# A third load buffer, chained key products and transposes, and a second bank for a gate, in a four-layer float32 kernel

## The chip, the cores and the metric

The kernel runs on one core of a Trainium2 chip. Its time is the device time of one execution in microseconds (us). The time before is the median of three runs, and one further execution was recorded by the hardware profiler; the rows below come from that one.

## The reference

Two blocks of two layers each are computed in float32 for 512 tokens of width 1024. The change touches mostly the first layer. It normalises the input, multiplies it with one wide matrix, and feeds the columns to a windowed attention and to a state space mixer; the outputs are gated, joined and projected.

```
def even_layer(hn, ...):
    q, k, v, gate_a, u, gate_b = split_cols(hn @ w_in, EVEN_SPLITS)   # 512,128,128,512,512,512
    q = rms_norm(q.reshape(bsz, L, 8, 64), q_g); k = rms_norm(k.reshape(bsz, L, 2, 64), k_g)
    att = swa_sink_attention(q, k, v, sinks, rel_bias) * silu(gate_a)
    ssm = s5_mixer(u, log_dt, a_re, ..., d_skip, glu_w, glu_b) * silu(gate_b)
    return concatenate([att, ssm], -1) @ w_out

def s5_mixer(u, ...):
    ab, f from exp(log_dt), a_re, a_im;  bb = f * b               # small complex tables
    x = associative_scan of x[l] = ab * x[l-1] + bb u[l]          # 32 groups, 64 states
    y = gelu(re(c x) + d_skip * u)
    h = y @ glu_w + glu_b
    return h[..., :512] * sigmoid(h[..., 512:])
```

The later layers are a top-k attention (layer 2), an attention with forget gates and one with dilated windows (layers 3 and 4, function `attn34`), the last two each followed by a convolutional feed-forward block. Between every two of these stands `h = h + out` and a root mean square norm.

## The kernel before

Each float32 product is made of three products of rounded parts (`mm3`, lines 227 to 229 and, through a `Chain`, line 361): a weight is loaded to a tile `raw` (line 211), ScalarE writes the rounded part `wh` (line 216), VectorE or GpSimd the remainder `wl` (line 217). `slab` does this for 8 x 128 rows by 256 columns in two parts. Tiles of one tag share a fixed number of buffers: two of `raw`, two pairs of `wh` and `wl`, two PSUM banks `acc`. `ring["lo"] = G` gives the remainder of a slab's second part to GpSimd in the state space stage.

The program is written in order, but a planner fixes the order of instructions on each engine from its own model of their lengths, by priority in the order of the text; `urgent` raises the priority. The engines then run their lists in order and wait on semaphores. `tc.issue_after(ins)` fixes that the instructions in its block stand behind `ins` on that engine; `Chain` does so for each TensorE instruction that passes through it, and so writes out an order by hand.

The first stage runs so: `norm_half(0)` normalises token blocks 0 and 1 (VectorE line 266 in two halves, then eight transposes on TensorE, line 288, and the split of the result, lines 291 and 292), with a few products on zeros that keep TensorE busy (`keep_warm`). `kv_half(0)` makes keys and values of these 256 tokens, turns them (line 505), normalises the keys (`head_norm`, lines 440 to 445, with a power on GpSimd, line 251), and turns them again (line 511). `norm_half(1)` and `kv_half(1)` follow for blocks 2 and 3, with the small tables of the state space model on VectorE between them. Then the products for `u2` (line 647), and the state space mixer in four quarters: `core_a(qu)` (lines 659 to 742; VectorE makes `zb`, lines 675 to 677, TensorE turns and multiplies it, VectorE makes `c7`, line 715, TensorE uses that at line 722) and `core_b(qu)` (lines 744 to 805; a scan on VectorE with the table `et`, TensorE's `yp`, line 780, then a gelu). The table `et` is built by doubling in `cmul_pow` (lines 571 to 574). The query products and the gates' products (`silu2`) stand behind in the text and fill TensorE in between as far as the planner puts them there.

The attention of layer 1 (lines 1050 to 1075) goes through units of a token block and a key head: `l1_scores`, one or two `glu_piece`s, `l1_values`, `l1_turn`. All its TensorE work but the norms' transposes goes through one `Chain`. `glu_piece(n)` makes half a gated unit in the PSUM bank `misc`, of which there is one: the even `n` end in a tanh on ScalarE (line 920), the odd ones in line 926 on VectorE. `finish` writes the output projection in quarters to `misc` (the last block's first half to `o`), then `norm_block` normalises the block, and four steps later its eight transposes are written, to the banks `misc` and `tps`, the last block's later still. `attn34` uses the same `finish` and chain; layer 2 uses `finish` without a chain.

Of the kernel before, what the change touches and what calls it, by code (L numbers as in the profile page):

```python
# [8 lines left out]
F32 = mybir.dt.float32  # L9
# [88 lines left out]
def _build(tc, nc, ctx, t, out, dbg, upto):  # L98
# [90 lines left out]

    ring = {"n": 0, "extra": None, "lo": V}  # L190

# [3 lines left out]

    def slab(src, r0, kc, pieces, wpool=None, parts=None):

        n = sum(p[1] for p in pieces)
        per = max(1, 1024 // n)
        pl = wpool  # L200
        if pl is None:
            ring["n"] += 1
            pl = ring["extra"] if ring["extra"] and ring["n"] % 3 == 0 else wp
        hi = pl.tile([128, WSZ], F32R, tag="wh", name="wh")[:, :kc * n].rearrange("p (k n) -> p k n", n=n)
        lo = pl.tile([128, WSZ], F32R, tag="wl", name="wl")[:, :kc * n].rearrange("p (k n) -> p k n", n=n)
        def part(k0, k1):
            raw = rawp.tile([128, 1024], F32, tag="raw", name="raw")[:, :(k1 - k0) * n].rearrange(
                "p (k n) -> p k n", n=n)
            o = 0
            for c0, w in pieces:  # L210
                nc.sync.dma_start(raw[:, :, o:o + w],
                                  src[r0 + k0 * 128:r0 + k1 * 128, c0:c0 + w].rearrange("(k p) n -> p k n", p=128))
                o += w
            eng = G if ring["lo"] is G and k0 > 0 else V
            with urgent() if evq[1] else nullcontext():
                A.activation(hi[:, k0:k1], raw, AF.Copy)  # L216
                eng.tensor_tensor(lo[:, k0:k1], raw, hi[:, k0:k1].bitcast(F32), op=OP.subtract)  # L217
        for k0 in range(0, kc, per):
            f = lambda k0=k0: part(k0, min(kc, k0 + per))
            if parts is None:  # L220
                f()
            else:
                parts.append(f)
        return hi, lo
# [56 lines left out]

    def to_x(xn, hdst, ldst, nk=8, tags=("tps", "tps"), view=lambda a: a):

        for half in range(nk // 4):
            ps = pst(tags[half])
            pv = ps.rearrange("p (k t) -> p k t", k=4)
            for k in range(4):
                turned[0] = PE.transpose(pv[:, k], xn[:, (half * 4 + k) * 128:(half * 4 + k + 1) * 128], ident).ins
# [5 lines left out]
    def norm_block(hb, gb, x, tb, tags=("tps", "tps"), pl=None, put_off=None):  # L294
        xn = (pl or nrm).tile([128, 1024], F32, tag="xn", name="xn")
        norm_scale(hb, gb, xn)
        sl = slice(tb * 128, (tb + 1) * 128)

        def rest():
            to_x(xn, lambda hf: x.h[hf][:, :, sl], lambda hf: x.l[hf][:, :, sl], tags=tags)  # L300
        if put_off:
            put_off(rest)
        else:
            rest()
# [142 lines left out]

    w = slab(w_in1, 0, 8, [(512, 256)])
    tmp = nrm.tile([128, 1024], F32, tag="xn", name="tmp")
    br = tmp[:, :512].rearrange("p (r g i) -> p r g i", r=2, g=16)  # L450
    for i, nm in enumerate(("ev_ssm_b_re", "ev_ssm_b_im")):
        for q in range(2):
            nc.sync.dma_start(br[q * 64:(q + 1) * 64, i],
                        t[nm][0].rearrange("(q g) p i -> q p g i", q=2)[q])
    crow = tmp[:, 512:].rearrange("p (r f x) -> p r f x", r=2, f=2)
    for i, nm in enumerate(("ev_ssm_c_re", "ev_ssm_c_im")):
        for hf in range(2):
            nc.sync.dma_start(crow[:, i, hf].rearrange("r (q p) -> r q p", q=2),
                              t[nm][0].rearrange("(q f g) o p -> f (g o) q p", q=2, f=2)[hf])
    mkd = pp.tile([128, 16], F32, name="mkd")  # L460
    nc.sync.dma_start(mkd, t["maskd"])
    qg = cst.tile([128, 4], F32, name="qg")
    for i, nm in enumerate(("ev_q_norm_g", "ev_k_norm_g")):
        for q in range(2):
            nc.sync.dma_start(qg[q * 64:(q + 1) * 64, i:i + 1], t[nm].rearrange("o d -> d o"))
    for i, nm in enumerate(("od_q_norm_g", "od_k_norm_g")):
        nc.sync.dma_start(qg[:, 2 + i:3 + i], t[nm].rearrange("o d -> d o"))
    qgs = cst.tile([128, 4], F32, name="qgs")
    V.tensor_copy(qgs, qg)
    V.tensor_scalar(qgs[:, 0:1], qg[:, 0:1], -0.125, None, op0=OP.mult)  # L470
    V.tensor_scalar(qgs[:, 2:3], qg[:, 2:3], -float(np.float32(128 ** -0.5)), None, op0=OP.mult)
    normed = []
# [12 lines left out]
    def norm_half(half):  # L485
        for tb in (2 * half, 2 * half + 1):
            normed.append(norm_block1(xin[tb], gb, x1, tb, n0, normed[-1] if normed else None))
            if half == 0:
                with tc.issue_after(turned[0]):
                    keep_warm(4)  # L490

    def kv_half(half):
        kvf = []
        for part in range(2):
            ps = acc()
            fm(ps[:, :256].rearrange("p (i j) -> p i j", i=4), w, part * 128, 128, xhalf(x1, half))
            f_ = n0.tile([128, 256], F32, tag=f"kvf{part}", name="kvf", bufs=1)
            evac(by_i(f_), ps[:, :256].rearrange("p (i j) -> p i j", i=4))
            kvf.append(f_)
        for q in range(2):  # L500
            tb = 2 * half + q
            sl = slice(tb * 128, (tb + 1) * 128)
            ps = sps()
            for part in range(2):
                PE.transpose(ps[:, part * 128:(part + 1) * 128], kvf[part][:, q * 128:(q + 1) * 128], ident)
            kn2 = pj.tile([128, 2, 2, 64], F32, tag="kn2", name="kn2", bufs=2)
            head_norm(ps[:, :128], 2, 64, [kn2[:, :, r] for r in range(2)])
            evac(vt[:, tb], ps[:, 128:256])
            tp = pst("ft")
            for i in range(2):  # L510
                PE.transpose(tp[:, i * 128:(i + 1) * 128], kn2[:, i].rearrange("p a d -> p (a d)"), ident)
            A.activation(kT[:, :, sl], tp[:, :256].rearrange("p (a t) -> p a t", a=2), AF.Copy, scale=qgs[:, 1:2])

    norm_half(0)

    def ctile():
# [7 lines left out]
    prmps = sps()  # L524
    with tc.issue_after(turned[0]):
# [103 lines left out]

    def bias_read(dst, h0, nh, m0, n):  # L630
# [6 lines left out]

    pst_.close()

# [243 lines left out]
    evq[1], ring["lo"] = False, V  # L883
    ssx.close()
# [25 lines left out]
    def glu_piece(n):  # L910
# [844 lines left out]
```

## Time and profile before

| | us |
|---|---|
| median of three runs | 1863.38 (1863.2 to 1865.21) |
| the profiled execution | 1865.96 |
| its span, first to last instruction | 1864.2 |
| TensorE busy in it | 1782.7 |
| mean granted clock of TensorE in it, 1 being full | 0.983 |

The span is what the views below divide; 1.8 us lie around it. Busy times of the engines overlap, so they do not add up to the span. The clock is granted at one of two levels, 1.0 or 0.5 of full speed, and a window's value is a mean of both.

### The profile page before, as it was taken

The page shows a single profiled execution, that of the slowest core. Times are in us where ns is not written, and L with a number is a line of the kernel's source. Part 1 is how long each engine was busy: PE and PEld are TensorE (multiplying, and loading weights), DVE is VectorE, ACT ScalarE, POOL GpSimd, SP SyncE. Part 2 cuts the span into 40 slices and gives each one's busy share as a digit, 9 for nine tenths or more (in the row PEclk, how much of TensorE's full clock was granted, in tenths as well). Part 3 has the DMA queues.
Part 4 walks back from the last instruction along what each step waited for, and adds up shares of the span by engine and source line. Part 5 has one row for each costly group of instructions (what it writes and reads, how often), then busy time and mean ns, then how long its engine had stood idle before and what let it go on. Part 6 is the DMA issues. An engine that isn't in the chain of part 4 may idle for free.

```text
span 1864.2 us, 27803 instructions
## 1 busy us (share of the span) xinstructions
PE 1782.7 (96%) x11134; PEld 1507.9 (81%) x11136; DVE 1036.1 (56%) x2110; ACT 735.8 (39%) x1460; POOL 152.5 (8%) x160
## 2 busy tenths in 40 slices
PE   7899899999999999899999999999999899999998
PEld 5777689878689886788888888889967888888886
DVE  6865475279855525655655562266466455555522
ACT  5333353353444335544433342233355344333421
POOL 3432101222120000000000000000000000000000
PEclk8889999999999999999999999999999999999999
DMA  5303222312513233003333323333410133332221
GB/s 166 117 12 109 96 91 64 91 58 68 163 46 120 84 116 97 1 2 104 112 92 91 91 74 118 103 125 96 132 46 1 37 113 99 103 93 80 101 91 68
DMA packets 187897, 161.73 MB, mean 87 GB/s; under 512 B 14568, under 2 KB 170320, under 8 KB 187768
## 3 DMA queue, kind: packets, MB, share of 16 engines
q1 hardware_dynamic: 181168, 144.30, 24.9%
q0 software_dynamic: 2784, 9.00, 1.6%
q10 hardware_dynamic: 3816, 6.66, 1.0%
q8 instruction: 88, 1.44, 0.3%
q14 instruction: 41, 0.34, 0.1%
HBM read 157.88 MB, written 4.74 MB: 87 GB/s over the span
## 4 chain that ended last, share of the span: by engine, by line
PE 74%; DVE 12%; ACT 4%; issue 4%; DMA 3%; POOL 2%; POOLq 0%; DVEq 0%; SPq 0%; ACTq 0%
PE acc L227 19%; PE acc L229 19%; PE acc L228 18%; PE misc L361 6%; PE o L361 3%; DVE wl L217 2%; PE tps L361 1%; PE spp L361 1%; ACT wh L216 1%; DVE isc L1198 1%; ACT p L1517 1%; PE misc L227 1%; DVE xn L266 1%; POOL rstd L251 1%; PE misc L228 1%
## 5 line engine op out<-in xcount | busy, mean ns | idle before, releaser
L217 DVE TENSOR_TENSOR wl<-raw,wh 128x1024 fp32r<-128x1024 f32 (+3 forms) x242 | 294.2, 1225 | 375.1 <-ACT wh L216 374.6
L216 ACT ACTIVATE wh<-raw 128x1024 fp32r<-128x1024 f32 (+2 forms) x262 | 270.2, 1044 | 490.4 <-PE acc L228 200.5
L227 PE MATMUL acc<-xh,wh 128*128 128x512 f32 (+2 forms) x1064 | 401.2, 379 | 3.9 <-ACT xh L291 3.9
L228 PE MATMUL acc<-xl,wh 128*128 128x512 f32 (+2 forms) x1064 | 401.0, 377 | 0.0
L229 PE MATMUL acc<-xh,wl 128*128 128x512 f32 (+2 forms) x1064 | 400.0, 376 | 0.0
L227 PEld LDWEIGHTS acc<-xh,wh 128*128 128x128 f32 (+1 forms) x1064 | 199.8, 189 | 43.7 <-ACT xh L291 4.6
L229 PEld LDWEIGHTS acc<-xh,wl 128*128 128x128 f32 (+1 forms) x1064 | 200.4, 188 | 39.2
L228 PEld LDWEIGHTS acc<-xl,wh 128*128 128x128 f32 (+1 forms) x1064 | 200.4, 188 | 38.4 <-DVE xl L292 0.2
L227 PE MATMUL acc<-wh,xh 128*128 128x256 f32 (+1 forms) x704 | 204.7, 291 | 1.6 <-ACT xh L291 1.4
L229 PE MATMUL acc<-wh,xl 128*128 128x256 f32 (+1 forms) x704 | 201.2, 286 | 0.8 <-DVE xl L292 0.8
L228 PE MATMUL acc<-wl,xh 128*128 128x256 f32 (+1 forms) x704 | 200.1, 285 | 0.0
L227 PEld LDWEIGHTS acc<-wh,xh 128*128 128x128 f32 x704 | 134.9, 192 | 9.8 <-issue 6.2
L229 PE MATMUL acc<-wh,gl 128*128 128x512 f32 x352 | 139.2, 395 | 0.0
L227 PE MATMUL acc<-wh,gh 128*128 128x512 f32 x352 | 138.5, 394 | 0.0
L228 PE MATMUL acc<-wl,gh 128*128 128x512 f32 x352 | 138.5, 393 | 0.0
L229 PEld LDWEIGHTS acc<-wh,xl 128*128 128x128 f32 x704 | 135.1, 192 | 1.4 <-DVE xl L292 1.2
L228 PEld LDWEIGHTS acc<-wl,xh 128*128 128x128 f32 x704 | 135.0, 192 | 0.2 <-issue 0.2
L264 POOL TENSOR_TENSOR rs<-ss,mhalf 128x1 f32<-128x1 f32 x32 | 17.7, 553 | 1398.8 <-DVE ss L262 1323.4
L361 PE MATMUL misc<-wh,ah 128*128 128x256 f32 x280 | 81.9, 293 | 3.6 <-DVE xl L292 2.2
L361 PE MATMUL misc<-wh,al 128*128 128x256 f32 x280 | 79.6, 284 | 2.0 <-DVE al L1556 2.0
L361 PE MATMUL misc<-wl,ah 128*128 128x256 f32 x280 | 79.0, 282 | 0.0
L228 PEld LDWEIGHTS acc<-wl,gh 128*128 128x128 f32 x352 | 66.1, 188 | 15.6
(1383 smaller groups left out, 3064.9 us busy)
## 6 DMA issues: line engine op xcount, KB each, us to landing
raw<-in_w_up_dram SPq DMA_DIRECT2D x176, 256.0 KB, 3.2
raw<-in_w_down_dram SPq DMA_DIRECT2D x44, 512.0 KB, 3.5
raw<-in_od_w_in_dram SPq DMA_DIRECT2D x24, 512.0 KB, 3.4
raw<-in_w_in_dil_dram SPq DMA_DIRECT2D x20, 512.0 KB, 3.6
raw<-in_ev_w_in_dram SPq DMA_DIRECT2D x18, 512.0 KB, 3.6
raw<-in_w_out_dram SPq DMA_DIRECT2D x16, 512.0 KB, 3.3
raw<-in_w_in_fox_dram SPq DMA_DIRECT2D x14, 512.0 KB, 4.1
raw<-in_ev_w_out_dram SPq DMA_DIRECT2D x8, 512.0 KB, 3.6
```

The lines of the kernel that those rows point to most:

```text
L216: A.activation(hi[:, k0:k1], raw, AF.Copy)
L217: eng.tensor_tensor(lo[:, k0:k1], raw, hi[:, k0:k1].bitcast(F32), op=OP.subtract)
L227: pe.matmul(ps, lh, rh, start=first, stop=False)
L228: pe.matmul(ps, lh, rl, start=False, stop=False)
L229: pe.matmul(ps, ll, rh, start=False, stop=last)
L251: G.tensor_tensor(r2[:, :n], r[:, :n], mhalf[:, :n], op=OP.pow)
L264: G.tensor_tensor(r, ss[:, 3:4], mhalf[:, :1], op=OP.pow)
L266: last = V.scalar_tensor_tensor(xn[:, hv[i]], hb[:, hv[i]], r, gb[:, hv[i]], op0=OP.mult, op1=OP.mult)
L361: self.last = op(*a, **k).ins
L1198: V.match_replace(out=s_, in_to_replace=m8_, in_values=s_, imm_value=-3e38)
L1517: A.activation(p2, src, AF.Exp, bias=nm[:, hd:hd + 1], scale=-1.0, accum_out=sm[:, hd:hd + 1])
```

## The change

Four things are done. In the state space stage each third part of a weight slab is loaded to a `raw` tile of a pool of its own (`rawx`); to make room, the pool `prep` is closed earlier, `mkd` and the key halves move to the pool `pj`, and the tanh of `silu2` shares the buffer `s_` of the gelu. The key slab's two splits are written behind `norm_half(0)`, and its remainders on VectorE stand behind the norm of block 1; `kv_half(1)`'s products, the first four `u2` products, and between those the turns and norms of `kv_half(1)` go through a chain `c1`. `glu_piece` 1 and 3 use the bank `o`. Where `finish` has a chain, the norms' transposes go through it and use two `tps` banks.

```
+    ring = {"n": 0, "extra": None, "lo": V, "raw": None, "rn": 0}
 ...
         def part(k0, k1):
-            raw = rawp.tile([128, 1024], F32, tag="raw", name="raw")[...]
+            ring["rn"] += 1
+            raw = (ring["raw"] if ring["raw"] and ring["rn"] % 3 == 0 else rawp).tile([128, 1024], ...)[...]
 ...
                 A.activation(hi[:, k0:k1], raw, AF.Copy)
-                eng.tensor_tensor(lo[:, k0:k1], raw, hi[:, k0:k1].bitcast(F32), op=OP.subtract)
+                with tc.issue_after(lo_after()) if lo_after else nullcontext():
+                    eng.tensor_tensor(lo[:, k0:k1], raw, hi[:, k0:k1].bitcast(F32), op=OP.subtract)
 ...
-    w = slab(w_in1, 0, 8, [(512, 256)])
+    kvparts = []
+    w = slab(w_in1, 0, 8, [(512, 256)], parts=kvparts, lo_after=lambda: normed[1])
+    ...
+    c1 = Chain()
+    def kv_half(half):
+        kvf, kn = [], {}
+        for part in range(2):
+            ps = acc()
+            fm(..., w, part * 128, 128, xhalf(x1, half), pe=c1 if half else PE)
+            f_ = pj.tile([128, 256], F32, tag="qn", name="kvf", bufs=2)
+            evac(by_i(f_), ...)
+            kvf.append(f_)
+        pe = c1 if half else PE
+        def norm(q):    # two transposes through pe, head_norm, evac of the values
+        def turn(q):    # two transposes through pe, ScalarE to kT
+        return [lambda: norm(0), lambda: norm(1), lambda: turn(0), lambda: turn(1)]
+    norm_half(0)
+    for f in kvparts:
+        f()
 ...
-    kv_half(0)
+    for f in kv_half(0):
+        f()
     norm_half(1)
 ...
-    kv_half(1)
+    kv_rest = kv_half(1)
 ...
+    pst_.close()
     ysx = ExitStack()
 ...
+    ring["raw"] = phase(ssx, "rawx")
 ...
-            tm(ps[:, :256], w, xk(x1, i * 128, i * 128 + 128))
+            tm(ps[:, :256], w, xk(x1, i * 128, i * 128 + 128), pe=c1)
+            if kv_rest:
+                kv_rest.pop(0)()
             evac(u2[:, cs_ * 16:(cs_ + 1) * 16, i, :], ...)
 ...
-        th_ = pl.tile([128, 512], F32, tag="th", name="th_", bufs=1)
+        th_ = pl.tile([128, 512], F32, tag="s_", name="s_")
 ...
-        w, ps = glu_w[cs_], pst("misc")
+        w, ps = glu_w[cs_], pst("o" if n in (1, 3) else "misc")
 ...
-                norm_block(h[:, tb], gb, x, tb, ("misc", "tps"), pl, lambda f: steps.later(4, f))
+                norm_block(h[:, tb], gb, x, tb, ("tps", "tps") if chain else ("misc", "tps"), pl,
+                           lambda f: steps.later(4, f), chain or PE)
```

## Rows read from the trace of the kernel before

**Rows 1.** The page's part 1: engine, busy us, share of the span, instructions.
```profile
PE 1782.7 (96%) x11134; PEld 1507.9 (81%) x11136; DVE 1036.1 (56%) x2110; ACT 735.8 (39%) x1460; POOL 152.5 (8%) x160
```

**Rows 2.** Windows: stretch, its length, busy us of PE, PEld, DVE, ACT, POOL, PEclk, DMA, GB/s.
```profile
45.00:52.00 7.00, 3.97 (x10) 1.20 (x11) 5.84 (x20) 2.28 (x6) 1.73 (x2) 0.71 0.43 143
52.00:76.00 24.00, 23.77 (x191) 23.48 (x191) 23.69 (x25) 4.47 (x9) 17.86 (x17) 0.94 0.37 112
76.00:82.00 6.00, 0.54 (x4) 0.35 (x3) 5.86 (x12) 3.18 (x5) 0.98 (x1) 0.72 0.51 170
...
113.00:130.00 17.00, 17.00 (x95) 14.36 (x94) 7.77 (x16) 3.48 (x6) 5.81 (x5) 0.50 0.00 1
...
222.00:226.00 4.00, 4.00 (x13) 2.88 (x11) 0.98 (x3) 0.00 (x0) 0.00 (x0) 0.57 0.00 0
```

**Rows 3.** Waits of PE from 0 to 232 us: us in total, times, longest.
```profile
PE tps L722 <- ACT bt L707: 5.5, 1, 5.5
PE ft L511 <- DVE kn L445: 3.6, 1, 3.6
```

**Rows 4.** Timeline of DVE: start, us, engine, line, operation, tiles, [idle before, releaser].
```profile
13.28 1.22 DVE L217 TENSOR_TENSOR wl<-raw,wh 128x1024 fp32r<-128x1024 f32 x1 [1.20 <-ACT wh L216]
...
15.67 1.23 DVE L217 TENSOR_TENSOR wl<-raw,wh 128x1024 fp32r<-128x1024 f32 x1 [0.56 <-ACT wh L216]
16.81 0.75 DVE L266 SCALAR_TENSOR_TENSOR xn<-xin,rs,gb 128x512 f32<-128x512 f32 x1
```

**Rows 5.** Timeline of PE, the first half's key products, first after the restart and last.
```profile
20.80 0.39 PE L228 MATMUL acc<-xl,wh 128*128 128x256 f32 x1
...
26.30 0.28 PE L229 MATMUL acc<-xh,wl 128*128 128x256 f32 x1
```

**Rows 6.** Timeline of DVE from 33 to 82 us: table doubling, two splits, the tile c7.
```profile
33.98 0.21 DVE L571 TENSOR_TENSOR ctmp<-pw 128x32 f32<-128x32 f32 x1
...
52.71 3.94 DVE L571 TENSOR_TENSOR ctmp<-et 128x32 f32<-128x32 f32 x1
...
65.39 5.41 DVE L571 TENSOR_TENSOR ctmp<-et 128x256 f32<-128x256 f32 x1
...
72.90 1.22 DVE L217 TENSOR_TENSOR wl<-raw,wh 128x1024 fp32r<-128x1024 f32 x1
...
81.41 0.28 DVE L715 TENSOR_TENSOR c<-sps,dm 128x128 f32<-128x128 f32 x1
```

**Rows 7.** Timeline of ACT from 78 to 82 us.
```profile
78.56 1.06 ACT L216 ACTIVATE wh<-raw 128x1024 fp32r<-128x1024 f32 x1 [8.80 <-DMA raw<-in_ev_w_in_dram]
...
81.11 1.08 ACT L707 ACTIVATE bt<-tps 128x512 f32<-128x512 f32 x2
```

**Rows 8.** Timeline of PE, the starts of gated-unit pieces 1 and 3.
```profile
221.42 0.51 PE L361 MATMUL misc<-yh,wh 128*128 128x512 f32 x1 [2.56 <-ACT th__2201 L920]
...
232.66 0.50 PE L361 MATMUL misc<-yh,wh 128*128 128x512 f32 x1 [1.73 <-ACT th__2259 L920]
```

**Rows 9.** Timeline of PE, two quarters of layer 1's output projection behind transposes.
```profile
299.90 0.38 PE L361 MATMUL misc<-wh,ah 128*128 128x256 f32 x1 [1.32 <-DVE ss L261]
...
313.39 0.39 PE L361 MATMUL misc<-wh,ah 128*128 128x256 f32 x1 [0.97 <-DVE xl L292]
```

**Rows 10.** Timeline of PE in layers 3 and 4, transposes of the norm and what follows.
```profile
790.10 0.66 PE L288 MATMUL tps<-ident,xn 128*128 128x128 f32 x4 [1.50 <-ACT pt__7978 L381]
792.00 0.55 PE L361 MATMUL misc<-wh,ah 128*128 128x256 f32 x1 [1.24 <-DVE xl L292]
...
842.13 0.55 PE L288 MATMUL tps<-ident,xn 128*128 128x128 f32 x3 [3.88 <-DVE xn L266]
...
1475.17 0.90 PE L288 MATMUL tps<-ident,xn 128*128 128x128 f32 x3 [3.88 <-DVE xn L266]
```

**Rows 11.** Timeline of DVE at 790 and 842 us.
```profile
790.94 0.41 DVE L379 COPY pt__7983<-tps 128x256 f32<-128x256 f32 x1
...
841.99 0.68 DVE L1556 TENSOR_TENSOR al<-o,ah 128x512 fp32r<-128x512 f32 x1
```

More of the change, by code (lines that the diff above doesn't have):

```diff
@@ L187, in urgent, with slab @@
         return tc.high_priority()
-    ring = {"n": 0, "extra": None, "lo": V}
+    ring = {"n": 0, "extra": None, "lo": V, "raw": None, "rn": 0}
     def ring_start(extra):
         ring["n"], ring["extra"] = 2, extra
-    def slab(src, r0, kc, pieces, wpool=None, parts=None):
+    def slab(src, r0, kc, pieces, wpool=None, parts=None, lo_after=None):
         n = sum(p[1] for p in pieces)
@@ L206, in part @@
         def part(k0, k1):
-            raw = rawp.tile([128, 1024], F32, tag="raw", name="raw")[:, :(k1 - k0) * n].rearrange(
+            ring["rn"] += 1
+            raw = (ring["raw"] if ring["raw"] and ring["rn"] % 3 == 0 else rawp).tile([128, 1024], F32, tag="raw", name="raw")[:, :(k1 - k0) * n].rearrange(
                 "p (k n) -> p k n", n=n)
@@ L280, in _build, with to_x @@
     turned = [None]
-    def to_x(xn, hdst, ldst, nk=8, tags=("tps", "tps"), view=lambda a: a):
+    def to_x(xn, hdst, ldst, nk=8, tags=("tps", "tps"), view=lambda a: a, pe=PE):
         for half in range(nk // 4):
@@ L287, in to_x @@
             for k in range(4):
-                turned[0] = PE.transpose(pv[:, k], xn[:, (half * 4 + k) * 128:(half * 4 + k + 1) * 128], ident).ins
+                turned[0] = pe.transpose(pv[:, k], xn[:, (half * 4 + k) * 128:(half * 4 + k + 1) * 128], ident)
             pv = view(pv)
@@ L292, in to_x, with norm_block @@
             V.tensor_tensor(ldst(half), pv, h_.bitcast(F32), op=OP.subtract)
-    def norm_block(hb, gb, x, tb, tags=("tps", "tps"), pl=None, put_off=None):
+    def norm_block(hb, gb, x, tb, tags=("tps", "tps"), pl=None, put_off=None, pe=PE):
         xn = (pl or nrm).tile([128, 1024], F32, tag="xn", name="xn")
@@ L446, in head_norm @@
                                 r.rearrange("p (h o) -> p h o", o=1).to_broadcast([128, nh, dh]), op=OP.mult)
-    w = slab(w_in1, 0, 8, [(512, 256)])
[L449 to L471, printed above, removed]
+    kvparts = []
+    w = slab(w_in1, 0, 8, [(512, 256)], parts=kvparts, lo_after=lambda: normed[1])
     normed = []
@@ L488, in norm_half @@
             if half == 0:
-                with tc.issue_after(turned[0]):
+                with tc.issue_after(turned[0].ins):
                     keep_warm(4)
+    c1 = Chain()
     def kv_half(half):
-        kvf = []
+        kvf, kn = [], {}
         for part in range(2):
             ps = acc()
-            fm(ps[:, :256].rearrange("p (i j) -> p i j", i=4), w, part * 128, 128, xhalf(x1, half))
-            f_ = n0.tile([128, 256], F32, tag=f"kvf{part}", name="kvf", bufs=1)
+            fm(ps[:, :256].rearrange("p (i j) -> p i j", i=4), w, part * 128, 128, xhalf(x1, half), pe=c1 if half else PE)
+            f_ = pj.tile([128, 256], F32, tag="qn", name="kvf", bufs=2)
@@ L498, in kv_half @@
             evac(by_i(f_), ps[:, :256].rearrange("p (i j) -> p i j", i=4))
             kvf.append(f_)
-        for q in range(2):
-            tb = 2 * half + q
-            sl = slice(tb * 128, (tb + 1) * 128)
+        pe = c1 if half else PE
+        def norm(q):
             ps = sps()
             for part in range(2):
-                PE.transpose(ps[:, part * 128:(part + 1) * 128], kvf[part][:, q * 128:(q + 1) * 128], ident)
+                pe.transpose(ps[:, part * 128:(part + 1) * 128], kvf[part][:, q * 128:(q + 1) * 128], ident)
@@ L506, in kv_half @@
             kn2 = pj.tile([128, 2, 2, 64], F32, tag="kn2", name="kn2", bufs=2)
             head_norm(ps[:, :128], 2, 64, [kn2[:, :, r] for r in range(2)])
-            evac(vt[:, tb], ps[:, 128:256])
+            evac(vt[:, 2 * half + q], ps[:, 128:256])
+            kn[q] = kn2
+        def turn(q):
+            sl = slice((2 * half + q) * 128, (2 * half + q + 1) * 128)
             tp = pst("ft")
             for i in range(2):
-                PE.transpose(tp[:, i * 128:(i + 1) * 128], kn2[:, i].rearrange("p a d -> p (a d)"), ident)
+                pe.transpose(tp[:, i * 128:(i + 1) * 128], kn[q][:, i].rearrange("p a d -> p (a d)"), ident)
@@ L512, in kv_half @@
             A.activation(kT[:, :, sl], tp[:, :256].rearrange("p (a t) -> p a t", a=2), AF.Copy, scale=qgs[:, 1:2])
+        return [lambda: norm(0), lambda: norm(1), lambda: turn(0), lambda: turn(1)]
     norm_half(0)
+    for f in kvparts:
+        f()
+    tmp = nrm.tile([128, 1024], F32, tag="xn", name="tmp")
+    br = tmp[:, :512].rearrange("p (r g i) -> p r g i", r=2, g=16)
+    for i, nm in enumerate(("ev_ssm_b_re", "ev_ssm_b_im")):
+        for q in range(2):
+            nc.sync.dma_start(br[q * 64:(q + 1) * 64, i],
+                        t[nm][0].rearrange("(q g) p i -> q p g i", q=2)[q])
@@ new lines, in _build @@
+    crow = tmp[:, 512:].rearrange("p (r f x) -> p r f x", r=2, f=2)
+    for i, nm in enumerate(("ev_ssm_c_re", "ev_ssm_c_im")):
+        for hf in range(2):
+            nc.sync.dma_start(crow[:, i, hf].rearrange("r (q p) -> r q p", q=2),
+                              t[nm][0].rearrange("(q f g) o p -> f (g o) q p", q=2, f=2)[hf])
+    mkd = pj.tile([128, 16], F32, name="mkd")
+    nc.sync.dma_start(mkd, t["maskd"])
+    qg = cst.tile([128, 4], F32, name="qg")
+    for i, nm in enumerate(("ev_q_norm_g", "ev_k_norm_g")):
+        for q in range(2):
+            nc.sync.dma_start(qg[q * 64:(q + 1) * 64, i:i + 1], t[nm].rearrange("o d -> d o"))
@@ L516, in ctile @@
+    for i, nm in enumerate(("od_q_norm_g", "od_k_norm_g")):
+        nc.sync.dma_start(qg[:, 2 + i:3 + i], t[nm].rearrange("o d -> d o"))
+    qgs = cst.tile([128, 4], F32, name="qgs")
+    V.tensor_copy(qgs, qg)
+    V.tensor_scalar(qgs[:, 0:1], qg[:, 0:1], -0.125, None, op0=OP.mult)
+    V.tensor_scalar(qgs[:, 2:3], qg[:, 2:3], -float(np.float32(128 ** -0.5)), None, op0=OP.mult)
     def ctile():
@@ L524, in _build @@
     prmps = sps()
-    with tc.issue_after(turned[0]):
+    with tc.issue_after(turned[0].ins):
         for i in range(3):
@@ L882, in _build @@
             silu2(sp_, gat[:, cs_ * 2 + q], ps)
-    evq[1], ring["lo"] = False, V
+    evq[1], ring["lo"], ring["raw"] = False, V, None
     ssx.close()
```

3 lines of the change are left out of this document (1 added, 2 removed).

## The prediction

> **What bounds the kernel now.** I read the page's busy shares first: TensorE is busy 96% of the span [rows 1], so an edit can only give back its idle time and the stretches at half clock. The windows come second. The reader should see that the idle time lies in few places: in 45 to 52 us TensorE works 3.97 of 7 us, and in 76 to 82 us 0.54 of 6, and that between these two VectorE is busy 23.69 of 24 us, with GpSimd at work in 17.86 of them [rows 2]. From 113 to 130 us TensorE is busy throughout, at a clock of 0.50. Third come the waits of TensorE, which name what ends the gaps: 5.5 us for the tile `bt` at line 722 and 3.6 us for `kn` at line 511 [rows 3]. The timelines of VectorE and ScalarE tell why those were late [rows 4, 6, 7], and TensorE's own timeline shows the gated unit and the transposes [rows 8 to 10]. All times are of the profiled execution, 1865.96 us, of which 1.8 lie around the span; it is 2.6 us above the median of 1863.38. I take the savings from it and subtract the same microseconds from the median.
>
> **The change part by part.**
>
> *The key slab behind the norms.* The norm's second half for block 1 stands at 16.81 us behind two remainders of 1.22 and 1.23 us, which themselves waited 1.20 and 0.56 us for ScalarE [rows 4]: 4.2 us that the order now moves behind it. The second remainder still ends at 15.67 + 1.23 = 16.90, since its data bound it, and the key products resume at 20.80 [rows 5]. With the norm out of the way they can resume near 16.9, up to 3.9 us earlier. Nothing is added; the slab's loads stay next to the inputs' on SP's queue, as no other load is written between. What may take the gain back is ScalarE's list, if a later split stands ahead of the next blocks' transposes there. So 0 to 3.9; I take 3, near the upper end, because the row's waits are plain and the products that follow run without gap from 20.80 to 26.30 [rows 5].
>
> *The second half's keys in a chain with the first `u2` products.* The 3.6 us wait for `kn` at line 511 [rows 3] blocked `u2` products that were ready; now two or three blocks of them stand between a norm and its turn. The clock in that window is 0.71, so of its 3.97 busy us some 3.97 x 0.29 = 1.2 are lost too [rows 2]: 4.8 at most. The new risk is the chain itself: if `kn` is late once more, the products queued behind it wait, at the price of the same row, 3.6. But the products then finish early in front of a VectorE that is full until 82 us [rows 2], and only what TensorE takes from its later work in the time won counts. So from -4.8 to +3.6; I take -2. The closing of `prep`, the new place of `mkd` and of the key halves cost nothing as instructions: the same ones run on the same engines. The shared buffer of `silu2` lets no gate go before the last gelu; the queries, not the gates, fill that time today.
>
> *The third load buffer.* ScalarE waited 8.80 us for a load, until 78.56, and the eviction of `bt` stood behind it at 81.11 [rows 7]. That load waited for a `raw` buffer, freed by the remainder that VectorE reached at 72.90 [rows 6]; with a third buffer the first part of the slab is there long before. The second part takes an old buffer and still waits for that remainder. What is late next is `c7`: it ends at 81.41 + 0.28 = 81.69 us [rows 6], and line 722 reads it also. If VectorE keeps its list, the 5.5 us are worth 0.1. If the planner, which sees the products of `u2` end earlier, moves `c7` ahead of the remainder and of the tables before it, all 5.5 and the half clock in 76 to 82 us [rows 2] may go, some 7. A third buffer adds no instruction, so below nothing there is only contention among loads, and the loads' share is 0.37 and 0.51 there [rows 2]. I take 3, in the middle, as the row does not tell what the planner does.
>
> *The second bank for pieces 1 and 3 of the gated unit.* Both waited for the tanh of the piece before, 2.56 and 1.73 us [rows 8], and behind the first the clock fell: 4.00 us at 0.57, 4.00 x 0.43 = 1.7 lost [rows 2]. Together 6.0. Piece 3 now waits for line 926 of piece 1, a score and a whole piece 2 earlier, and the first values for that of piece 3, a score and a piece earlier; that work covers both. If VectorE is late there, one of the waits stays and the gain is 2.6. I take 5.5.
>
> *The transposes in the chains.* In layer 1 two quarters of the projection waited 1.32 and 0.97 us for transposes to leave `misc` [rows 9]. They now leave `tps`, which no turn needs any more at that point: 2.3 gained. In layers 3 and 4 the largest waits, 3.88 us each [rows 10], are for a norm of the next block; but the product that follows needs `al`, which VectorE makes at 841.99 [rows 11], so it could start 0.1 us earlier at most, at 842.67, and the gap stays. In the other place the transposes waited 1.50 us for one `tps` bank; the second of the two banks is free only at 790.94 + 0.41 = 791.35 [rows 11], 1.25 us later than they started, while the 1.24 us behind them [rows 10] go. These cancel. So for layers 3 and 4 I take 0, between 5 us gained (3.88 once, with a clock that stays up) and 7.5 lost (1.25 for each of the six blocks there that pass the chain).
>
> Sum: 3 + 2 + 3 + 5.5 + 2.3 = 15.8, say 16 us: 1865.96 - 16 = 1850 for an execution like the profiled one, and 1863.4 - 16 = 1847 for the median.
>
> **The rivals.**
>
> *VectorE holds the state space stage.* The buffer does not act, as only every third part uses it and the stage's end is VectorE's. For it: VectorE has no gap from 52 to 82 us [rows 2], and its table products are stretched while GpSimd works: 3.94 us for a 128x32 product that took 0.21 before, and 5.41 for one of 128x256 [rows 6]. Against it: the first remainders come earlier, so VectorE's list starts earlier. Then the second and third terms are 0 and the first is 1.5: 1.5 + 5.5 + 2.3 = 9, 1854 us. The Trainium skill, page "SBUF — State Buffer", section "Who interferes with whom", says that VectorE and GpSimd share a pair of ports under an exclusive lock, so that a VectorE instruction with two SBUF inputs and a GpSimd instruction that reads SBUF exclude each other. By that rule the stretched rows are work that no load buffer can shorten, and the sum would be this rival's; the trace agrees so far as the stretching goes, and does not show whether the order on VectorE stays.
>
> *The clock stays up.* From 113 to 130 us TensorE is busy 17.0 us at 0.50 [rows 2]: 8.5 us would go if query products filled the gaps ahead of it. For it: the queries' weights arrive earlier with the third buffer. Against it: VectorE sets those gaps, and nothing in the diff touches `core_b`. 16 + 8.5 = 24.5 gives 1839.
>
> *The hand-written order holds TensorE.* Slower: in layers 3 and 4 each of the six blocks' transposes stands right behind a turn that has taken both `tps` banks, and nothing may pass it. Price: 1.50 for the first bank, 1.25 more for the second, and a clock that falls behind the gap, some 1.7 as behind the gated unit: 4.4 a block, 27 in all, against 16 gained: 1874. It decides from 16 / 6 = 2.7 us a block. For it: the wait of 1.50 is there already [rows 10]. Against it: most of these blocks have score and projection work queued that keeps the clock, and the planner had its own stalls at the same spots.
>
> **How the numbers follow.** Forecast 0.48 (own range 1842 to 1853), VectorE holds 0.27, clock 0.15, slower 0.10. About 0.2% (3.7 us) is what a measurement of this kernel can tell from no change. Faster by more than that means below 1859.7: nearly all of the forecast, four fifths of the second case and all of the third, 0.47 + 0.21 + 0.15 = 0.83; slower 0.09; the rest, 0.08, is within. The range runs from 1832, into the clock's case with a few more of the upper ends, to 1861, past the second case with half of the gated unit's gain; some 0.07 lies below and 0.12 above.
>
> **What would show it.** Right: no wait of line 361 in `misc` for the first and third piece's tanh; line 511 without a wait and the `u2` products over by about 62 us; the key products running by 18 us; no wait of ScalarE above 2 us for a slab in 60 to 82 us; no wait behind transposes in layer 1. Of the third buffer's term: where `c7` stands on VectorE, before or behind the last table product. Wrong: line 722 starting at 79 us or later would make the second rival true; waits at line 288 or 361 for `tps` of over 2.7 us a block the last; a clock of 1.0 through the quarters of the mixer the third.

## The result and the profile after

The changed kernel takes 1877.68 us (median of 4 runs, 1872.41 to 1880.23), the kernel before on the same chip 1863.60 (4 runs): ratio 1.0056, 95% interval [1.0037, 1.0075]. It is slower; the forecast was 1847 us. The profiled execution took 1872.41 us, 6.45 more than that of before. (The ratio is not the quotient of the two medians, which is 1.0076, or 14.1 us; the ratios with their intervals are used from here on.)

The page's part 1, as in [rows 1]: TensorE still is busy 95%, so the loss again lies in a few places.

```profile
PE 1780.0 (95%) x11136; PEld 1509.6 (81%) x11136; DVE 1032.9 (55%) x2110; ACT 736.7 (39%) x1460; POOL 157.1 (8%) x160
```

The windows of [rows 2], in the changed kernel. From 52 to 76 us TensorE fell from 23.77 busy us to 11.84, at a clock of 0.71; VectorE is as full as before. The stretch from 113 to 130 us went the other way: its clock is 0.90, not 0.50.

```profile
45.00:52.00 7.00, 5.17 (x24) 5.17 (x25) 7.00 (x6) 0.00 (x0) 6.84 (x5) 0.54 0.49 145
52.00:76.00 24.00, 11.84 (x83) 11.60 (x82) 23.19 (x46) 4.54 (x11) 13.69 (x11) 0.71 0.42 133
76.00:82.00 6.00, 6.00 (x51) 6.00 (x51) 1.23 (x1) 3.03 (x5) 2.50 (x1) 0.98 0.24 76
113.00:130.00 17.00, 13.88 (x166) 11.27 (x165) 12.24 (x23) 4.16 (x11) 8.60 (x10) 0.90 0.00 1
```

The waits of TensorE from 0 to 242 us, against [rows 3]. The 5.5 us for `bt` and the 3.6 for `kn` are gone; in their place stand 12.2 us for `kn` and 5.0 for `wl` in the chain c1 (line 364 issues all chained work), and 5.0 for a tanh of the gated unit. The wait for `zz` is not new: it was 6.4 us in three parts before.

```profile
PE ft L364 <- DVE kn L448: 12.2, 1, 12.2
PE yp L799 <- DVE zz L788: 5.0, 2, 2.6
PE acc L364 <- DVE wl L220: 5.0, 1, 5.0
PE misc L364 <- ACT th__2205 L940: 5.0, 1, 5.0
```

*Why `kn` was late.* The timelines of VectorE and of GpSimd, 55 to 71 us. VectorE reduces the squares at 55.23; the reciprocal root on GpSimd (line 254) comes only at 61.92, behind tables and the split of a load at 59.62; and `kn` itself stands behind nearly the whole doubling of `et` (from 57.56) and runs at 70.71, 8 us after its root was there. The wait for `wl`, which ends at 46.83, has a similar look: two remainders from 44.70 took VectorE 4.07 us beside GpSimd's table work, and 2.35 in e10 below, where the wait is gone.

```profile
55.23 0.27 DVE L445 TENSOR_REDUCE ssh<-sq 128x2 f32<-128x128 f32 x1
...
57.56 1.20 DVE L841 COPY et<-uu 128x32 f32<-128x32 f32 x1
58.79 3.26 DVE L587 TENSOR_TENSOR ctmp<-et 128x32 f32<-128x32 f32 x1
...
70.71 0.88 DVE L448 TENSOR_TENSOR kn<-sps,rstd 128x128 f32<-128x128 f32 x4
```

```profile
59.62 2.35 POOL L220 TENSOR_TENSOR wl<-raw,wh 128x1024 fp32r<-128x1024 f32 x1
61.92 0.73 POOL L254 TENSOR_TENSOR rstd<-rstd,mhalf 128x2 f32<-128x2 f32 x1
```

*Why the tanh was late.* GpSimd's timeline shows that the bias tile `sb` is requested at 223.32 us, after 21.06 us of waiting for the last gate (line 886), whose input is the tanh tile `s_`:

```profile
223.32 1.62 POOL L649 DMA_DIRECT2D sb<-bias_d  x2 [21.06 <-DVE gat L886]
229.16 2.13 POOL L913 TENSOR_TENSOR sb<-sb,swam 128x1024 f32<-128x1024 f32 x1 [4.22 <-DMA sb<-bias_d]
```

In the kernel before the same two steps, with no wait for a gate:

```profile
194.94 1.62 POOL L631 DMA_DIRECT2D sb<-bias_d  x2
199.91 4.25 POOL L894 TENSOR_TENSOR sb<-sb,swam 128x1024 f32<-128x1024 f32 x2 [3.36 <-DMA sb<-bias_d]
```

The scores' minimum needs `sb`, four exponentials on ScalarE need the minimum, and the first tanh of the gated unit stands behind them in ScalarE's list (its timeline, changed kernel), though its product had been ready since 227.65:

```profile
233.66 0.51 ACT L1019 ACTIVATE s<-s,nm 128x256 f32<-128x256 f32 x1 [11.45 <-DVE nm L1013]
...
235.74 0.67 ACT L940 ACTIVATE th__2205<-misc,gbc 128x512 f32<-128x512 f32 x1
```

TensorE's timeline, against [rows 8]: piece 1 now starts without a wait in its own bank, and piece 2 waits in `misc` for the tanh of piece 0.

```profile
227.48 0.40 PE L364 MATMUL o<-yh,wh 128*128 128x512 f32 x1
...
236.46 0.65 PE L364 MATMUL misc<-yh,wh 128*128 128x512 f32 x1 [4.95 <-ACT th__2205 L940]
```

Two marks divide the span into three stretches for all that follows: the first gate's product on VectorE (line 886, 867 before) and the first score product of layer 2 (line 1254, 1233 before), each the first start in the view of its line. For the changed kernel:

```profile
L886 DVE SCALAR_TENSOR_TENSOR gbt<-s__1869,acc x1: 1072/1072/1072, 182.0 to 182.0; 128x512 f32<-128x512 f32 x1
...
L1254 PE MATMUL sps<-kT,qT x64: 273/434/697, 494.8 to 572.2; 128*128 128x512 f32 x16, 128*128 128x384 f32 x16, 128*128 128x256 f32 x16, 128*128 128x128 f32 x16
```

| profiled execution of | first gate at, us | gate to layer 2 | layer 2 to the end |
|---|---|---|---|
| before | 174.7 | 310.1 | 1379.4 |
| after | 182.0 | 312.8 | 1375.7 |
| a_again (after once more) | 179.9 | 315.0 | 1379.4 |
| e1_no_order | 179.7 | 311.9 | 1379.4 |
| e2_turns_late | 175.9 | 313.8 | 1381.5 |
| e3_th_xn | 178.1 | 305.2 | 1379.2 |
| e5_norms_first | 178.1 | 311.4 | 1377.4 |
| e6_both | 172.0 | 303.6 | 1380.7 |
| e7_both_misc | 169.8 | 310.2 | 1382.3 |
| e8_both_trout | 170.9 | 304.4 | 1378.6 |
| e9_both_two | 173.4 | 305.1 | 1379.2 |
| e10_both_chain | 172.1 | 304.3 | 1376.4 |
| e11_tr_l1 | 175.4 | 305.3 | 1380.4 |
| b1_shared | 172.7 | 318.6 | 1379.6 |

The first and last columns scatter: code that is the same up to the first gate reached it between 169.8 and 175.4 us (e6, e7, e8, e11), and the last column differs by 3.7 us between two executions of one kernel (after, a_again). The middle one is the steadiest, and within groups of the same edits agrees to 2 us (4 where the bias tile is late).

### The profile page after: what moved, and what is told of

It reads as the page before. It is cut to its first block, busy times and chain, and to the rows that moved or that the text cites. A ratio compares the mean times of both kernels' runs of the same rounds, so it can differ in the third digit from the quotient of the medians.

```text
span 1870.5 us, 27815 instructions
## 1 busy us (share of the span) xinstructions
PE 1780.0 (95%) x11136; PEld 1509.6 (81%) x11136; DVE 1032.9 (55%) x2110; ACT 736.7 (39%) x1460; POOL 157.1 (8%) x160
## 4 chain that ended last, share of the span: by engine, by line
PE 77%; DVE 12%; ACT 4%; DMA 3%; issue 3%; POOL 1%; POOLq 0%; DVEq 0%; SPq 0%; ACTq 0%
PE acc L230 19%; PE acc L232 19%; PE acc L231 19%; PE misc L364 6%; PE o L364 3%; PE tps L364 2%; DVE wl L220 2%; PE acc L364 1%; PE spp L364 1%; DVE isc L1219 1%; ACT p L1538 1%; DVE xn L269 1%; PE misc L230 1%; PE o L1278 1%; PE misc L231 1%
## 5 line engine op out<-in xcount | busy, mean ns | idle before, releaser
L230 PE MATMUL acc<-xh,wh 128*128 128x512 f32 (+2 forms) x1048 | 396.1, 379 | 0.5 <-ACT xh L294 0.5
L231 PE MATMUL acc<-xl,wh 128*128 128x512 f32 (+2 forms) x1048 | 395.7, 378 | 0.0
L232 PE MATMUL acc<-xh,wl 128*128 128x512 f32 (+2 forms) x1048 | 394.8, 377 | 0.0
L230 PE MATMUL acc<-wh,xh 128*128 128x256 f32 (+1 forms) x640 | 186.2, 291 | 0.9 <-ACT xh L294 0.9
L232 PE MATMUL acc<-wh,xl 128*128 128x256 f32 (+1 forms) x640 | 182.4, 285 | 0.4 <-DVE xl L295 0.4
L231 PE MATMUL acc<-wl,xh 128*128 128x256 f32 (+1 forms) x640 | 182.7, 286 | 0.0
L230 PEld LDWEIGHTS acc<-wh,xh 128*128 128x128 f32 x640 | 122.9, 192 | 8.0 <-issue 5.8
L232 PEld LDWEIGHTS acc<-wh,xl 128*128 128x128 f32 x640 | 122.9, 192 | 0.7 <-DVE xl L295 0.7
L231 PEld LDWEIGHTS acc<-wl,xh 128*128 128x128 f32 x640 | 123.0, 192 | 0.3 <-issue 0.2
L230 PEld LDWEIGHTS acc<-wh,gh 128*128 128x128 f32 x352 | 66.4, 189 | 15.1
```

Of the source, the lines that this page charges most:

```text
L230: pe.matmul(ps, lh, rh, start=first, stop=False)
L231: pe.matmul(ps, lh, rl, start=False, stop=False)
L232: pe.matmul(ps, ll, rh, start=False, stop=last)
```

## The experiments

Twelve kernels, four on one chip at a time, each compared with the kernel before on that chip (medians 1866.35, 1867.41 and 1866.26 us). The theory: two side effects of the diff cost the time, the place at which the key norms are written (too late for VectorE), and the tanh buffer shared by `silu2` (the bias tile has to wait for it). The rivals: the written order c1 itself, VectorE's tables, the second bank, the chained transposes.

**a_again.** The changed kernel, unaltered.

> The changed kernel once more, unaltered, as the measure for the others on this chip and to see how far its own times scatter: its four times ran from 1872.4 to 1880.2 us. Both theories: 1877, ratio to before 1.005 to 1.008. Of the scatter one theory says that it lies in a stage that runs once (the state space stage, 45 to 230 us), another that it is the clock in the later layers; the profile of this copy against the first one tells in which stage the starts differ by more than 1 us.

1875.70 us, ratio 1.0040 [1.0024, 1.0056]. The change costs between 0.24 and 0.75% over both chips. The profile has the same waits (12.53 us for `kn`, 6.91 for `wl`, 6.78 for the tanh).

**e1_no_order.**

```diff
-    c1 = Chain()
+    c1 = PE
```

> c1 is made the plain tensor engine, so that the second half's key products, norms and turns have no written order against the u2 products; all else as after. Theory A (the fixed order puts turn(0) ahead of ready products while kn is late on VectorE): the 12.2 us wait for kn goes, the u2 products end near 76 instead of 88.6, the first gate product starts 6 to 9 us earlier than 175, total 1868 to 1871. Rival B (VectorE's tables hold the stage, the order is innocent): the wait moves to the first L741 product, the first gate product stays within 2 us, total 1875 or more. Rival C (bias reads behind the last gate, gated unit): untouched by this, its 5 us wait of the gated unit stays in both.

1874.68 us, 1.0044 [1.0031, 1.0058]: no gain. Without a written order the planner puts the turn ahead of `u2` products too: TensorE waits 13.45 us for `kn`, which VectorE reaches at 75.38 (the line below is the sum of three waits, from 0 to 242 us). The theory that the run was meant to show (the written order makes TensorE wait) fell: the order c1 is not what makes `kn` late, nor does taking it away help.

```profile
PE ft L500 <- DVE kn L448: 16.2, 3, 13.5
```

**e2_turns_late.** The order kept, the turns behind the last `u2` product.

```diff
-            if kv_rest:
+            if len(kv_rest) > 2:
                 kv_rest.pop(0)()
...
-    dump("u2", u2)
+    [f() for f in kv_rest]
```

> The fixed order is kept, only the two turns move behind the last u2 product. Theory A: 12.2 us of wait gone, u2 over by 76 to 78, first gate product 166 to 169, total 1868 to 1871, as in the run without the order. Rival B (VectorE holds the stage): as after, 1875 or more. If the order as such costs (and not the place of the turns), this run stays slow and the one without the order gets fast.

1873.28 us, 1.0032 [1.0020, 1.0044], not told apart from a_again. The wait of the turn is gone and another took its place: TensorE waits 9.9 us for ScalarE to clear a bank of `u2`, and ScalarE, in its fixed list, stands at the evacuation of `vt` for 9.89 us, behind `kn` again. So whatever depends on the late `kn` blocks one engine or the other, and moving the turn alone is no cure (the first gate, at 175.9, is 2 to 6 us earlier than in the other kernels with a late `kn`, which is within that column's scatter). ScalarE's timeline:

```profile
73.16 0.48 ACT L384 ACTIVATE vt<-sps 128x128 f32<-128x128 f32 x2 [9.89 <-DVE kn L448]
```

**e3_th_xn.** Only the place of the gates' tanh.

```diff
-        th_ = pl.tile([128, 512], F32, tag="s_", name="s_")
+        th_ = nrm.tile([128, 1024], F32, tag="xn", name="th_")[:, :512]
```

> The tanh buffer of the gates (silu2) is taken from the norm tile xn instead of from the buffer s_ of the state space stage; third load buffer, order, banks and chains stay. Theory A (the bias tile sb lies on the memory of s_, so its read waits for the last gate): the bias read is issued near 201 instead of 223, the scores' minimum and the four exponentials come at once, the first tanh is not held behind them, piece 2's wait of 4.95 us goes and the clock with it, the first output projection quarter comes 5 to 7 us earlier, total 1871 to 1873, with the state space stage unchanged (first gate product 175). Rival D (the second bank itself reorders ScalarE so that the exponentials stand ahead of the tanh whatever the bias does): wait stays, total 1877.

1865.92 us, 0.9995 [0.9985, 1.0005]: 0.45% less than the changed kernel beside it, some 8 us. The bias tile is requested at 198.24 without a wait, the tanh waits of 5 to 7 us are gone, and the middle column falls from 312.8 and 315.0 to 305.2. GpSimd's timeline:

```profile
198.24 1.62 POOL L649 DMA_DIRECT2D sb<-bias_d  x2
202.63 4.25 POOL L913 TENSOR_TENSOR sb<-sb,swam 128x1024 f32<-128x1024 f32 x2 [2.78 <-DMA sb<-bias_d]
```

**e5_norms_first.** As e1, and the norms and turns written at once, as before.

```diff
-    kv_rest = kv_half(1)
+    kv_rest = [f() for f in kv_half(1)] and []
```

> No written order (c1 plain) and the second half's norms and turns written straight behind its key products, as in the kernel before; everything else as after, the shared s_ buffer too. Theory A2 (not the order on TensorE but the place in the program makes kn late: written behind u2 blocks, its arithmetic falls behind the et doubling on VectorE and behind cp on GpSimd): kn is over by 50 us, no wait for it above 4 us, u2 over by 66 to 74, the first gate 7 to 10 us before that of the run with the order taken out alone (179.7), total 1865 to 1868. Rival B (the table work of VectorE holds the stage however kn stands): first gate within 3 us of 179.7, total 1873 or more.

1866.57 us, 0.9995 [0.9981, 1.0009]: 0.49% less than e1, some 9 us. `kn` is over at 48.2, ahead of `et`, and no wait for it exceeds 1.5 us; the `bt` wait of before is back with 4.80. The first gate came only 1.6 us earlier than in e1, so this profile alone misses the number forecast; the times and the six kernels below with the same edit show the step. VectorE's timeline:

```profile
46.58 0.28 DVE L448 TENSOR_TENSOR kn<-sps,rstd 128x128 f32<-128x128 f32 x1
47.48 0.69 DVE L448 TENSOR_TENSOR kn<-sps,rstd 128x128 f32<-128x128 f32 x3 [0.62 <-POOL rstd L254]
49.13 0.20 DVE L841 COPY et<-uu 128x32 f32<-128x32 f32 x1
```

**e6_both.** The edits of e3 and e5 together.

> The same, and the tanh buffer of the gates in the norm tile, as in the run that freed the bias read. If the two causes are independent, the gains add: 1866 - 8 = 1857 to 1859, ratio to before 0.995 to 0.997. If the earlier gates only make the scores wait for something else (the bias tile's read or the gate weights), 1862 or more.

1856.81 us, 0.9944 [0.9929, 0.9958]: the gains add, and this beats both kernels. The waits of TensorE up to 232 us hold no tanh and no late `kn`; the pause ahead of line 741 is there as it was at line 722, 5.4 us here.

```profile
PE yp L799 <- DVE zz L788: 6.5, 3, 2.7
PE tps L741 <- issue: 5.4, 1, 5.4
PE acc L230 <- ACT u L384: 3.5, 1, 3.5
PE ft L500 <- DVE kn L448: 3.0, 3, 1.4
```

**e7_both_misc.** e6 without the second bank.

```diff
-        w, ps = glu_w[cs_], pst("o" if n in (1, 3) else "misc")
+        w, ps = glu_w[cs_], pst("misc")
```

> As the run with both causes removed, but with all pieces of the gated unit in the bank misc, as before. My recorded step says that the second bank is worth 5.5 us (2.6 to 6): this run 5 to 6 us slower than its base, with waits of 2.6 and 1.7 us for the tanh of pieces 0 and 2 back. Rival: the second bank is worth nothing since the first out-projection waits for the last piece's arithmetic anyway: within 1 us.

1865.55 us, 0.9991 [0.9978, 1.0004], 0.47% more than e6; the middle column rises by 6.6 us against e6 and by 5.5 against the mean of the five kernels with bank, chains and an own tanh buffer (304.7). Both waits of [rows 8] are back. TensorE's timeline:

```profile
216.08 0.50 PE L364 MATMUL misc<-yh,wh 128*128 128x512 f32 x1 [2.25 <-ACT th__2205 L940]
...
227.27 0.50 PE L364 MATMUL misc<-yh,wh 128*128 128x512 f32 x1 [1.68 <-ACT th__2263 L940]
```

**e8_both_trout.** e6 with the transposes of the norms outside the chains (line 956 as before).

```diff
-                norm_block(h[:, tb], gb, x, tb, ("tps", "tps") if chain else ("misc", "tps"), pl,
-                           lambda f: steps.later(4, f), chain or PE)
+                norm_block(h[:, tb], gb, x, tb, ("misc", "tps"), pl,
+                           lambda f: steps.later(4, f))
```

> As the run with both causes removed, but with the transposes of a block's norm outside the chains, as before. My recorded step says 2.3 us slower in layer 1 and nothing in layers 3 and 4: 2 to 3 us slower than its base. Rival (the order holds TensorE in layers 3 and 4): from the first to the last L1628 product the copies with the transposes in the chains took 634 to 638 us and the kernel before 632.7, so 2 to 5 us come back there and the total is 0 to 3 us faster than its base.

1857.85 us, 0.9953 [0.9935, 0.9970]: not told apart from e6, and the middle column is 304.4. In layer 1 the chained transposes take away the waits of [rows 9], 1.3 and 1.0, and those of 0.5 and 0.3 us behind them, and bring one of 2.5 for the norm of the last block. The transposes of that block are not chained themselves (line 291, not 364): in the changed kernel they stand ahead of layer 2's first products, and in e8 behind those of 309.07 to 318.06 us. TensorE's waits from 280 to 345 us in the changed kernel are this one line:

```profile
PE tps L291 <- DVE xn L269: 2.5, 1, 2.5
```

**b1_shared.** The kernel before with the shared buffer alone.

```diff
-        th_ = pl.tile([128, 512], F32, tag="th", name="th_", bufs=1)
+        th_ = pl.tile([128, 512], F32, tag="s_", name="s_")
```

> The kernel before with one word changed: the gates' tanh buffer is the state space stage's s_ instead of a buffer of its own. Theory A (memory): the bias tile sb now lies on s_, its read is issued after the last gate, near 214 instead of 194.9 us; the first exponentials come 5 to 8 us late, hold the first tanh and the second piece's product behind it; the gated unit loses 5 to 8 us, total 5 to 8 us slower than before. Rival (the late bias read costs only where the second bank o is used, since with misc alone the piece waits for the tanh anyhow): within 2 us of before.

1875.96 us, 1.0042 [1.0029, 1.0055]. This one word makes the kernel before as slow as the changed one: the middle column grows by 8.5 us, and the wait for the first tanh from 2.56 to 9.12. GpSimd's and TensorE's timelines:

```profile
214.07 1.62 POOL L631 DMA_DIRECT2D sb<-bias_d  x2 [21.07 <-DVE gat L867]
```

```profile
227.23 0.80 PE L361 MATMUL misc<-yh,wh 128*128 128x512 f32 x1 [9.12 <-ACT th__2201 L920]
```

**e9_both_two.** e6 without the third load buffer.

```diff
-    ring["raw"] = phase(ssx, "rawx")
+    ring["raw"] = None
```

> As the run with both causes removed, without the third load buffer. My recorded step says 3 us (0 to 7) for it: this run 3 us slower than its base (1856.8), with a wait of ScalarE for a load and the first L741 product later. Rival (VectorE holds the stage, the recorded first rival): within 1.5 us, c7 within 1 us of its place at 83.4 us. A third possibility is that the buffer hurts, since c7 stands 2 to 9 us later in every run that has it: 1 to 3 us faster.

1861.26 us, 0.9965 [0.9948, 0.9981]; e6 has 0.9944 with an interval that overlaps. ScalarE waits 10.07 us for a weight's load again, as in [rows 7], and 2.83 in e6; but `c7` is at 84.2 against 83.4 and the first gate at 173.4 against 172.0. So the buffer acts on ScalarE; what it is worth the times leave open, between -2 and 10 us by the far ends of the two intervals (0.9948 less 0.9958 and 0.9981 less 0.9929, of 1866). ScalarE's timeline of e9:

```profile
81.93 1.06 ACT L218 ACTIVATE wh<-raw 128x1024 fp32r<-128x1024 f32 x1 [10.07 <-DMA raw<-in_ev_w_in_dram]
```

**e10_both_chain.** e6 with the written order kept (c1 a chain).

> As the run with both causes removed, but with the written order c1 kept on TensorE for the second half's products, norms and turns, which now come in one piece ahead of the u2 products. If the place of the norms in the program is the whole cause, this is within 2 us of its base (1856.8), with kn over by 52 us. If the written order itself costs, the turns hold the u2 products for 2 to 5 us after the key products and the total is 3 us or more slower.

1857.24 us, 0.9944 [0.9930, 0.9958], the same as e6. Here the turns do hold the `u2` products for 5.25 us, and no cost shows: VectorE is busy 23.62 of the 24 us from 52 to 76 and `c7` stands at 81.2 us. The wait (from 26 to 130 us) and the window:

```profile
PE ft L364 <- DVE kn L448: 5.3, 1, 5.3
```

```profile
52.00:76.00 24.00, 24.00 (x191) 24.00 (x191) 23.62 (x27) 4.85 (x10) 18.68 (x17) 0.93 0.46 143
```

**e11_tr_l1.** e6 with the transposes chained in layer 1 alone.

> As the run with both causes removed, with the chained transposes in layer 1 alone. The run without any of them was 1.0 us slower (not told apart) than its base. My recorded step says layer 1 gains 2.3 and layers 3 and 4 nothing: within 1 us of the base. Rival (layers 3 and 4 lose 2 us: 635.0 us from the first to the last L1628 product against 633.1 without): 1 to 3 us faster than the base.

1857.78 us, 0.9947 [0.9930, 0.9965]: not told apart from e6. In sum layers 3 and 4 neither gain nor lose by the chained transposes, as far as these times can tell (5 us gained to 7 lost, by the far ends of the two intervals).

## Why the prediction was wrong

The direction was wrong, and for two things that the prediction looked at and priced at nothing or at too little.

- *The shared tanh buffer: the step that failed first.* The prediction asked only whether a gate could start ("lets no gate go before the last gelu") and found it harmless, and the first gate is indeed no later in b1 (172.7 us) than before (174.7). It did not ask who comes later to that memory. The bias tile is opened when the stage closes; it had found free memory and now waits for the last gate. Price: 8.3 us (mean of the middle column over the five kernels with the shared buffer, the second bank and the chains, after, a_again, e1, e2 and e5, 313.0, less 304.7), shown both ways by e3 and b1. That the two tiles overlap in address is read from the releaser (line 886, the last reader of `s_`) and from its going when the tanh moved; no view prints addresses.
- *The second half's keys: -2 forecast, between -4.8 and +3.6.* The mechanism of the upper end was named (the products queued behind a late `kn` wait), its size was not: 12.2 us instead of 3.6. I took from [rows 3] how late `kn` had been and let it stand. But writing the norm behind a `u2` block moves all of its arithmetic, on VectorE and GpSimd too, and there it landed behind the doubling of `et`. Mean first gate of the three kernels with the norms so written and c1 untouched (after, a_again, e3): 180.0; of the seven with the norms in place (e5 to e11): 173.1. That is 6.9 us, in a column that scatters; by the times, e3 against e10, which differ in this edit alone, 0.51% or 9.5. The written order on TensorE, which I had in view, costs nothing that these runs can tell (e1 against a_again, e10 against e6).
- *The key slab behind the norms: -3.* Right at its place: the key products run at 17.70 instead of 20.80, as forecast, and the last ends at 24.27 instead of 26.58. No run takes this step out by itself.

```profile
17.70 0.73 PE L230 MATMUL acc<-xh,wh 128*128 128x256 f32 x2
...
23.99 0.28 PE L232 MATMUL acc<-xh,wl 128*128 128x256 f32 x1
```

- *These 2.3 us, the keys and the third buffer together: 8 forecast in the state space stage.* With the two side effects gone the first gate stands at 173.1 on average, against 174.7 and 172.7 in the two kernels that have none of the three (before and b1): between 0.4 lost and 1.6 won. This speaks for the first rival, VectorE holds the stage, though the times leave the buffer's own worth open (e9). `c7` lies between 80.4 and 85.0 us in all seven, 81.41 in [rows 6], whether loads come early (e6) or late (e9), whether the `u2` products are held (e10) or not; and that rival's sign came (it is called the second there, counting the forecast): the product of line 722, 741 now, starts at 80.8 to 85.4 us in all seven, not before 79. The Trainium skill's page "SBUF — State Buffer", section "Who interferes with whom", which I had set beside this rival, says that a VectorE instruction with two SBUF inputs and a GpSimd instruction that reads SBUF exclude each other. The trace agrees: the 128x32 product of line 587 took 3.26 us beside GpSimd's work (58.79 us, after) and the same kind 0.21 in [rows 6], where GpSimd stood idle. That this is why no load buffer shortens the stage, no run shows.
- *The clock from 113 to 130 us*, the second rival's stretch, was 0.90 instead of 0.50 in after, e6 and e10 alike, but that is not the diff's doing: b1, the kernel before but for the tanh buffer, shows 0.90 too (the line below). Nor is much won by it: from the first `c7` to the first gate it is 93.3 us in before and 91.5 in b1, 91.7 in after, and 87.6 to 93.6 in the seven (90.1 on average).

```profile
113.00:130.00 17.00, 16.07 (x138) 13.32 (x140) 12.31 (x25) 6.84 (x12) 7.17 (x6) 0.90 0.00 1
```

- *The gated unit: -5.5 forecast.* Right, and right in size once the bias tile is early: 5.5 us in the middle column (e7), 0.47% or 8.8 us by the times, whose intervals allow 3.7 to 14. In the changed kernel it was hidden: both pieces with the new bank start without a wait, and piece 2 pays for the late tanh.
- *The transposes in layer 1: -2.3 forecast.* The waits went as said and 2.5 us for `xn` came, so nothing is left: 310.2 with chains (e7) and 310.1 without (before), 304.4 without (e8) and 304.7 with them. The step looked only at the chained transposes and left out the last block's, which are not chained: the new list has them wait for their norm ahead of layer 2's ready products. *Layers 3 and 4: 0*, right in sum: the wait for `xn` of 3.88 in [rows 10] became one of 3.45 for `al`, as argued, and the last column shows no trend. Within that column two parts may cancel. From the first to the last product of line 1628 (1607 before; layer 4's attention lies between), the ten kernels with chained transposes took 634.5 to 638.2 us and the four without 632.7 to 634.8, means 636.3 and 633.4: 2.9 us lost. Ahead of it, from the first score product of layer 2 on, it is 364.3 to 370.7 against 369.2 to 372.0, means 367.6 and 370.5: 2.9 us won, or chance, since these ranges overlap. So the slower rival had the sign for layer 4, but far less than its six blocks at 4.4 us. The view of line 1628 in after, then in e8:

```profile
L1628 PE MATMUL sps<-ident,cr x8: 232/232/255, 860.9 to 1495.4; 44*128 44x44 f32 x8
L1628 PE MATMUL sps<-ident,cr x8: 232/232/255, 844.9 to 1478.1; 44*128 44x44 f32 x8
```

In sum, from the marks: 8.3 + 6.9 lost by the two side effects, 5.5 won by the bank, nothing to 2 won in the state space stage: 8 to 10 us slower, against 7 to 11 by the two ratios (0.40 and 0.56%; the medians give 9.4 and 14.1). Without the side effects the same diff is 0.56% faster (e6, e10), 10.5 us. That this is near the first rival's 9 is partly luck: 2.3 of the 9 were for the transposes in layer 1, which gave nothing.

## What to carry to other kernels

When a scratch tile is merged with another one to save space, look up which tile of the next phase gets that memory, and who waits for it: here one changed line cost 0.42%. When a step is moved in the program to give one engine a better order, follow its arithmetic on every other engine's list too; the matmul order was harmless, the place of a 0.9 us VectorE step behind 13 us of table work was not. And price a bank, a buffer or an order only together with what stands in front of it in the other engine's list: a gain of 5.5 us was there all the time, behind an exponential that waited for a load.

## What the runs showed of the hardware

Half-clock stretches fall differently in the same code. e6 and e10 differ only in `c1`, ahead of the first gate. Yet from the first score product of layer 2 to the first `cr` transpose in the feed-forward of layer 3 (line 1628) it took 370.6 us (475.6 to 846.2) in the one and 364.3 (476.4 to 840.7) in the other. Windows of 40 us show where: of the nine from the first mark on, e6 has four at less than full clock and e10 one (the four rows of e6, then the one of e10).

```profile
475.60:515.60 40.00, 37.86 (x223) 27.66 (x221) 30.70 (x86) 24.30 (x54) 11.38 (x21) 0.96 0.55 164
555.60:595.60 40.00, 38.35 (x304) 37.49 (x303) 23.16 (x50) 17.34 (x36) 1.65 (x3) 0.96 0.43 133
755.60:795.60 40.00, 35.01 (x313) 29.75 (x312) 24.30 (x95) 21.34 (x74) 0.55 (x1) 0.96 0.00 1
795.60:835.60 40.00, 35.37 (x318) 31.99 (x317) 22.66 (x61) 17.62 (x47) 1.10 (x2) 0.93 0.06 17
```

```profile
756.40:796.40 40.00, 35.75 (x325) 29.82 (x325) 25.69 (x100) 20.70 (x73) 0.55 (x1) 0.96 0.01 2
```

Lost clock makes 40 x (0.04 + 0.04 + 0.04 + 0.07) = 7.6 us in e6 and 40 x 0.04 = 1.6 in e10, so 6.0 of the 6.3 us, as far as values rounded to 0.01 can tell. What makes the clock fall in one run and not in the next stays open. It is not the only scatter: two executions of one kernel, after and a_again, agree in this stretch (366.1 and 366.3 us) and differ by 3.2 from the first to the last product of line 1628 (634.5 and 637.7), though every window of 80 us there has the same clock in both. Sixteen executions of the kernel before on one chip lie between 1862.89 and 1871.55 us, 0.5% apart. So a single run of such a kernel says little of a change of that size, and the marks above were needed to price the parts.
